# Decay rows repeated in DRAM and loaded by half heads, in a hybrid encoder layer

## The chip, the cores and the metric

The kernel runs on one core of a Trainium2 chip. The time is the device time of one execution in microseconds (us); for the kernel before the median of 3 runs is 810.5 us (810.26 to 810.57). One further execution was recorded by the hardware profiler; every duration below is of that execution. Engines are named as in the profile: PE is the TensorE matmul, PEld its weight load, DVE the VectorE, ACT the ScalarE, POOL the GpSimd, SP the SyncE, which here only issues transfers.

## The reference

One encoder layer in float32 over two sequences of 256 tokens, width 1024. From one joint projection come three branches: a bidirectional gated DeltaNet (8 heads, chunks of 64), a multi-head latent attention (MLA, 8 heads) and a cross-attention into a memory of 256 tokens. Each branch is gated and projected, the three are summed with sigmoid gates, projected and added to the input. The change works on the decay matrices of the first branch and on the order of work around them:

```python
gc = jnp.cumsum(g ..., axis=-1)                    # per head and direction
decay = jnp.exp(jnp.where(lower, gc[..., :, None] - gc[..., None, :], -jnp.inf))
lmat = jnp.einsum("nbhck,nbhek->nbhce", kb, kc) * decay * (1.0 - eye)
t_inv = lax.linalg.triangular_solve(lmat + eye, ...)
...
q_pe = _rope(q_pe, pos)
q_full = jnp.concatenate([q_nope, q_pe], axis=-1)
o_mla = _blocked_attention(q_full, k_full, v_mla, (D_NOPE + D_ROPE) ** -0.5)
```

So each head and each direction (forward, backward) needs exp(row of gc minus column of gc) under a triangular mask, times the products of the head's keys (kk), and then a triangular solve.

## The kernel before

Both sequences are handled together, as 512 columns. Each 128x128 block of a weight is used three times: weights and activations are split into a rounded part ("h": wh_, hh) and a remainder ("l": wl_, hl), and a product is hh·wh, hl·wh and hh·wl. A weight is therefore loaded (SP, L229, `wr_`), rounded (ACT, L241, `wh_`) and its remainder taken (DVE, L243, `wl_`) before PE can use all of it (L274). Two raw buffers and two of each part hold some two weights ahead.

There are three stages. In **front**, the memory branch and MLA run; between their products lie "fills", products that belong to other branches (the q, k, v of the DeltaNet `gm_qkv`, and its gates). In **middle**, a small planner (`weave`) puts the DeltaNet's heads among the remaining fills: it keeps a clock of PE time, each chain of work (heads coming in, two lanes of solves, heads going out, the norm) says with `yield cost, distance` how much PE time its step took and how much must pass before its next step, and fills take the time in between. PE follows the order that the planner wrote; DVE, ACT, POOL and SP get theirs from a scheduler with priorities. In **back** come the last projections. On each engine the order is fixed at build time: an instruction that waits holds up all behind it on that engine.

SP and ACT issue the transfers. As the built program shows, each transfer carries one of eight semaphores (DMAHW0 to DMAHW7), given out in turn over both engines, and a transfer waits until the one before it on the same semaphore has landed.

What the change touches:

- `d_r` (2 x 32 x 2 x 384 f32 in DRAM, L635 and L636): the rows of gc, for each direction, 4 rows per head. They are written in front.
- `decay_in` (L946): per head two tiles `e` of 128 x 768 (one per direction), each filled by four loads in which one row of `d_r` is repeated on 32 partitions: 8 loads per head, 64 in all. Two such buffers.
- `decay_mask` (POOL, L966) masks the triangles, four calls per head; `decay_exp` (ACT, L974) takes the exponent, eight calls per head; `gdn_in` makes the products kk (PE, L1008) and multiplies (DVE, L1018: `ne` from `e` and kk).
- `gdn_solve` goes through the triangular solve in steps that are 6.5 apart in the planner's time, `gdn_norm` multiplies by a row `rob` read back from DRAM (DVE, L1190) 10 after its load.
- `mla_rope` (called for half of MLA's heads at a time) rotates the position part of the queries on DVE, splits it, writes it to DRAM (L694, L695: `d_q`) and loads it back in another layout (L697, L700: `qs`). MLA's first product with it is `s_a<-ks,qs` (L335).
- In MLA, `pl_a` (DVE, L252) is the remainder of the transposed probabilities, `oa` (L370) the product with the values.

Of the kernel before, what the change touches and what calls it, by code (L numbers as in the profile page):

```python
# [7 lines left out]
F32 = mybir.dt.float32  # L8
# [173 lines left out]
class Layer:  # L182
    def __init__(self, tc, A):
        self.tc, self.nc, self.A = tc, tc.nc, A
# [39 lines left out]
    def weight(self, src, n, name, pool=None, into=None):  # L224
# [15 lines left out]
        with self.tc.high_priority(offset=60):  # L240
            self.wround = nc.scalar.activation(hi[:, :n], raw[:, :n], AF.Copy).ins  # L241
            lo = place("wl_", "wl")
            self.wsplit = nc.vector.tensor_tensor(lo[:, :n], raw[:, :n], hi[:, :n].bitcast(F32),  # L243
                                                  op=ALU.subtract).ins
        return hi, lo

    def split(self, src, hi, lo, scale=1.0):
# [3 lines left out]
        if isinstance(scale, float) and scale == 1.0:  # L251
            nc.vector.tensor_tensor(lo, src, hi.bitcast(F32), op=ALU.subtract)  # L252
# [72 lines left out]
    def attend(self, h, s, score, scale, vs, op, name):  # L325
# [39 lines left out]
        self.split(tp, hi, lo)  # L365
        n = 0
# [311 lines left out]
    def mla_rope(self, g):  # L678
# [6 lines left out]
        for j, (p1, p2, op) in enumerate(((pa, pb, ALU.subtract), (pb, pa, ALU.add))):  # L685
            t, u = self.tb("rt"), self.tb("ru")
# [5 lines left out]
            self.split(t, hi, lo)  # L692
# [8 lines left out]
        self.qs = qs1, qs2  # L701

# [237 lines left out]
    def decay_in(self, hh):  # L940
        es = []
        for d in range(2):
            e = self.pg.tile([P, 2, 384], F32, tag="e", bufs=2, name=f"e{hh}{d}")
            for a in range(4):
                src = self.d_r[d, 4 * hh + a:4 * hh + a + 1].rearrange("a s i -> a (s i)")
                self.nc.sync.dma_start(e[32 * a:32 * a + 32].rearrange("p s i -> p (s i)"), src.to_broadcast([32, 768]))  # L946
            es.append(e)
        return es
# [11 lines left out]
    def decay_mask(self, es):  # L960
        for d, e in enumerate(es):

            o = 128 if d else 0
            sg = -1 if d else 1
            for r in (slice(o, o + 128), slice(256, 384)):
                self.nc.gpsimd.affine_select(out=e[:, :, r], in_=e[:, :, r], pattern=[[0, 2], [sg, 128]],  # L966
                                             compare_op=ALU.is_ge, fill=NEG, base=0, channel_multiplier=-sg)

    def decay_exp(self, hh, d, e):
        for s in range(2):  # L970
            for cp in range(2):
                cch = cp if d == 0 else 1 - cp
                r = slice(0, 256) if cp == 0 else slice(256, 384)
                self.nc.scalar.activation(e[:, s, r], e[:, s, r], AF.Exp,  # L974
                                          bias=self.ngcl[:, d, 2 * s + cch, hh:hh + 1])

    def gdn_in(self, hh):
# [5 lines left out]
        es, vt = self.decay_in(hh), self.value_in(hh)  # L983
# [8 lines left out]
        yield 0.0, 10.0 if hh else 7.0  # L992
        self.decay_mask(es)
        for d in range(2):
            yield 0.0, 3.0
            with self.tc.issue_after(self.wround):
                self.decay_exp(hh, d, es[d])
        yield 0.0, 2.0
        v3 = vt.rearrange("p (t d) -> p t d", t=4)
        ne = pg.tile([P, 2, 2, 2, 384], F32, tag="ne", bufs=3, name=f"ne{hh}")  # L1000
        for s in range(2):
            pc = []
            hi, lo = hl[s]
            for cch in range(2):
# [5 lines left out]
                yield 0.65, 5.0 * cch  # L1010
            for d in range(2):
                for cp in range(2):
# [6 lines left out]
                        ne[:, :, d, s, r], es[d][:, s, r].unsqueeze(1).to_broadcast([P, 2, n]),  # L1019
                        cc[:, d, w:w + 1], kin, ALU.mult, ALU.mult)  # L1020
        nc.gpsimd.tensor_tensor(v3, v3, nk[:, 4 * h:4 * h + 4].unsqueeze(2).to_broadcast([P, 4, P]), op=ALU.mult)  # L1021
# [3 lines left out]
    def gdn_solve(self, hh):  # L1025
# [72 lines left out]
        for cp in range(2):  # L1098
            if cp == 1:
# [11 lines left out]
                yield 0.9, 6.5  # L1111
# [9 lines left out]
            yield 0.45, 6.5  # L1121
# [8 lines left out]
            yield 0.45, 6.5  # L1130
# [7 lines left out]
            yield 0.45, 6.5  # L1138
# [43 lines left out]
    def gdn_norm(self, hh):  # L1182
# [5 lines left out]
        yield 0.0, 6.0 if hh == 7 else 10.0  # L1188
# [506 lines left out]
```

## Time and profile before

| | before |
|---|---|
| median of 3 runs | 810.5 us |
| profiled execution, its own time | 810.69 us |
| span in the profile, first to last instruction | 808.9 us |
| mean granted PE clock | 0.998 |
| PE busy | 793.3 us, 98% |
| PEld busy | 699.5 us, 86% |
| DVE busy | 567.0 us, 70% |
| ACT busy | 448.9 us, 55% |
| POOL busy | 146.2 us, 18% |
| SP's queue of transfers, share of 16 DMA engines | 44.9% |
| ACT's queue of transfers | 0.8% |

Busy times are sums over instructions; the span is what counts, and 1.8 us of the execution's time lie outside it. The page divides the span into 40 slices, follows the chain of work that ended last, and groups instructions by line. The list of waits says, per engine, for what its instructions stood idle; the timeline gives single instructions with the idle time ahead of them in brackets and what ended it; a table of windows gives each engine's busy time within a stretch.

### The profile page before, as it was taken

The numbers are of one execution on the slowest core, as the hardware profiler recorded it, in microseconds if no ns is written. First come the engines' busy times: TensorE is split into PE (matmuls) and PEld (weight loads), VectorE is DVE, ScalarE is ACT, GpSimd is POOL, SyncE is SP. The second block draws the span as 40 slices with busy tenths as digits, with TensorE's granted clock in tenths as the row PEclk, the third lists the DMA queues.
The fourth block names the chain that finished last, engine by engine and source line by source line (L and its number), as shares of the span: only waits on it lengthen the run. The fifth ranks groups of instructions, "written<-read, shape, count | busy, mean of one in ns | idle before, by whom it ended". The sixth has DMA issues, their size and how long they took to land.

```text
span 808.9 us, 13180 instructions
## 1 busy us (share of the span) xinstructions
PE 793.3 (98%) x4822; PEld 699.5 (86%) x4822; DVE 567.0 (70%) x957; ACT 448.9 (55%) x895; POOL 146.2 (18%) x135
## 2 busy tenths in 40 slices
PE   9999999999999999999999999999999999999996
PEld 7888898889898889988888888788888888888885
DVE  7796358687699999668599998767644654455543
ACT  6765455456565566647666657576655552222332
POOL 0200111000010002074031137213110002223221
PEclk9999999999999999999999999999999999999999
DMA  8422222552417525355334454747444557354532
GB/s 324 170 75 103 92 87 72 183 158 72 118 59 221 173 95 161 130 157 158 130 111 130 140 147 154 203 137 192 135 132 131 182 188 262 128 196 147 186 104 105
DMA packets 68913, 118.20 MB, mean 146 GB/s; under 512 B 23664, under 2 KB 31216, under 8 KB 68848
## 3 DMA queue, kind: packets, MB, share of 16 engines
q1 hardware_dynamic: 67552, 115.00, 44.9%
q10 hardware_dynamic: 1296, 2.36, 0.8%
q8 instruction: 38, 0.62, 0.3%
q14 instruction: 27, 0.22, 0.1%
HBM read 98.24 MB, written 19.09 MB: 145 GB/s over the span
## 4 chain that ended last, share of the span: by engine, by line
PE 87%; DVE 6%; DMA 3%; ACT 2%; issue 1%; SPq 0%; POOL 0%; DVEq 0%; POOLq 0%; ACTq 0%
PE gm_g L274 15%; PE gm_qkv L274 13%; PE gm_z L274 7%; PE gm_bm L274 5%; PE gm_za L274 5%; PE y L1321 4%; PE gm_be L274 3%; PE gm_qm L274 3%; PE gm_km L274 3%; PE gm_bg L274 3%; PE o L1158 2%; PE gm_bg L1288 2%; PE kk L1008 2%; PE vm L426 2%; PE gm_qn L274 2%; PE gm_cq L274 2%
## 5 line engine op out<-in xcount | busy, mean ns | idle before, releaser
L775 DVE SCALAR_TENSOR_TENSOR kq<-cz,prm,kq 128x510 f32<-128x510 f32 (+1 forms) x64 | 52.7, 823 | 3.8 <-ACT kq L768 2.9
L274 PE MATMUL gm_qkv<-hh,wh_qkv 128*128 128x512 f32 x192 | 48.0, 384 | 1.3 <-ACT wh_qkv L241 1.3
L274 PE MATMUL gm_g<-hh,wl_g 128*128 128x512 f32 x192 | 48.9, 385 | 0.0
L274 PE MATMUL gm_g<-hh,wh_g 128*128 128x512 f32 x192 | 48.6, 386 | 0.0
L274 PE MATMUL gm_qkv<-hl,wh_qkv 128*128 128x512 f32 x192 | 48.1, 384 | 0.0
L274 PE MATMUL gm_g<-hl,wh_g 128*128 128x512 f32 x192 | 47.8, 384 | 0.0
L274 PE MATMUL gm_qkv<-hh,wl_qkv 128*128 128x512 f32 x192 | 47.4, 383 | 0.0
L243 DVE TENSOR_TENSOR wl_g<-wr_g,wh_g 128x1024 fp32r<-128x1024 f32 x24 | 29.5, 1227 | 19.6 <-PE gm_g L274 10.7
L243 DVE TENSOR_TENSOR wl_qkv<-wr_qkv,wh_qkv 128x1024 fp32r<-128x1024 f32 x24 | 30.7, 1281 | 16.4 <-PE gm_qkv L274 6.4
L1018 DVE SCALAR_TENSOR_TENSOR ne<-e,cc,kk 128x512 f32<-128x512 f32 (+1 forms) x64 | 35.5, 608 | 8.7 <-PE kk L1008 6.1
L274 PEld LDWEIGHTS gm_qkv<-hh,wh_qkv 128*128 128x128 f32 x192 | 35.6, 190 | 6.2 <-ACT wh_qkv L241 1.7
L274 PEld LDWEIGHTS gm_qkv<-hh,wl_qkv 128*128 128x128 f32 x192 | 36.0, 189 | 4.8
L274 PEld LDWEIGHTS gm_g<-hl,wh_g 128*128 128x128 f32 x192 | 35.7, 189 | 4.7
L274 PEld LDWEIGHTS gm_qkv<-hl,wh_qkv 128*128 128x128 f32 x192 | 35.7, 190 | 4.7
L274 PEld LDWEIGHTS gm_g<-hh,wl_g 128*128 128x128 f32 x192 | 35.4, 190 | 4.5
L274 PEld LDWEIGHTS gm_g<-hh,wh_g 128*128 128x128 f32 x192 | 35.2, 190 | 4.4
L1321 PE MATMUL y<-wh_wo,mh 128*128 128x512 f32 (+1 forms) x144 | 37.8, 356 | 0.0
L1263 POOL TENSOR_TENSOR mg<-mg,lg 128x512 f32<-128x512 f32 x16 | 28.0, 1761 | 50.6 <-DVE lg L1262 29.1
L241 ACT ACTIVATE wh_g<-wr_g 128x1024 fp32r<-128x1024 f32 x24 | 25.3, 1055 | 20.2 <-PE gm_g L274 13.8
L241 ACT ACTIVATE wh_qkv<-wr_qkv 128x1024 fp32r<-128x1024 f32 x24 | 25.4, 1057 | 19.7 <-PE gm_qkv L274 4.9
L990 POOL TENSOR_TENSOR kl<-kq,kh 128x512 fp32r<-128x512 f32 x16 | 22.6, 1418 | 53.3 <-ACT kh L988 50.7
L1021 POOL TENSOR_TENSOR vs<-vs,ns 128x512 f32<-128x512 f32 x8 | 8.4, 1049 | 127.1 <-DVE rs_a L352 84.9
(453 smaller groups left out, 2189.5 us busy)
## 6 DMA issues: line engine op xcount, KB each, us to landing
wr_g<-in_w_dram SPq DMA_DIRECT2D x24, 512.0 KB
wr_qkv<-in_w_dram SPq DMA_DIRECT2D x24, 512.0 KB
e<-d_r SPq DMA_DIRECT2D x64, 96.0 KB
wr_z<-in_w_dram SPq DMA_DIRECT2D x12, 512.0 KB
d_g<-gt_g SPq DMA_DIRECT2D x16, 256.0 KB
wr_za<-in_w_dram SPq DMA_DIRECT2D x8, 512.0 KB
lg<-d_g SPq DMA_DIRECT2D x16, 256.0 KB
wr_bm<-in_w_dram SPq DMA_DIRECT2D x8, 512.0 KB
```

The source lines that it names most:

```text
L241: self.wround = nc.scalar.activation(hi[:, :n], raw[:, :n], AF.Copy).ins
L243: self.wsplit = nc.vector.tensor_tensor(lo[:, :n], raw[:, :n], hi[:, :n].bitcast(F32), op=ALU.subtract).ins
L274: nc.tensor.matmul(pairs(ps[:m]), a[:, k * m:(k + 1) * m], turns(xs[k][j]), start=n == 0, stop=n == 3 * nk - 1)
L426: nc.tensor.matmul(pairs(vps[tb]), ms[k][a][:, t], turns(b[:, :512]), start=k == 0 and i == 0, stop=k == 7 and i == 2)
L775: nc.vector.scalar_tensor_tensor(ys, zs, self.cw[:, f, m:m + 1], ys, ALU.mult, ALU.add)
L990: nc.gpsimd.tensor_tensor(lo, src, hi.bitcast(F32), op=ALU.subtract)
L1008: nc.tensor.matmul(pairs(ps), a[:, k], turns(b), start=i == 0, stop=i == 2)
L1018: nc.vector.scalar_tensor_tensor(ne[:, :, d, s, r], es[d][:, s, r].unsqueeze(1).to_broadcast([P, 2, n]), cc[:, d, w:w + 1], kin, ALU.mult, ...
L1158: nc.tensor.matmul(out, ub[:, d, s, cp], rhs, start=n == 0, stop=n == 3)
L1263: nc.gpsimd.tensor_tensor(self.merged[d], self.merged[d], gt, op=ALU.add)
L1288: nc.tensor.matmul(pairs(ps), a[:, k * P:(k + 1) * P], turns(self.xg[k][j]), start=n == 0, stop=False)
L1321: nc.tensor.matmul(pairs(ps), xs[2 * j + q][a][:, t], turns(b[:, q * 512:(q + 1) * 512])[:, c0 // 2:c1 // 2], start=j == 0 and n == 0, sto ...
```

## The change

1. **Rows repeated in DRAM.** A new DRAM tensor `d_e` (2 x 8 x 128 x 2 x 384 f32) holds each head's four rows, each repeated 32 times. `decay_rows` fills it with 16 transfers from DRAM to DRAM, two per head, issued on ACT's queue. In the code it stands in the loop over MLA's heads.
2. **Tiles of half a head.** `e` becomes 128 x 384, one per head, sequence and direction: 32 loads of 192 KB in place of 64 of 96 KB, and four buffers in place of two (the same memory). Loads, masks and exponents become planner chains of their own (`decay_loads`, `decays`), half a head ahead of the products. The mask of a tile is one call on two blocks; their number per head stays four, that of the exponents eight.
3. **Distances.** From one kk to the next 5.0 becomes 6.5; the steps of the solve 6.5 to 7.2; the norm's row 10 to 12.
4. **MLA's rotation in two.** `mla_rope` becomes a generator: the first half of the rotation is made where all of it was, the second later, between the query products that follow; its split is put after the last weight rounding ahead of it in the program.
5. **One weight held back.** At the start of middle, the first weight remainder (`wl_`) is put after the last `pl_a` on DVE (`self.hold`).
6. Part 1 of the `xa` tiles moves from the e buffers to others and is loaded from another point on; the `xe` loads move one fill earlier.

The number and kind of PE's products stay as they are.

```diff
@@ weight
-            self.wsplit = nc.vector.tensor_tensor(lo[:, :n], raw[:, :n], hi[:, :n].bitcast(F32),
-                                                  op=ALU.subtract).ins
+            with nullcontext() if self.hold is None else self.tc.issue_after(self.hold):
+                self.wsplit = nc.vector.tensor_tensor(lo[:, :n], raw[:, :n], hi[:, :n].bitcast(F32),
+                                                      op=ALU.subtract).ins
+            self.hold = None
...
@@ mla_rope
         for j, (p1, p2, op) in enumerate(((pa, pb, ALU.subtract), (pb, pa, ALU.add))):
+            if j:
+                yield
...
-            self.split(t, hi, lo)
+            with self.tc.issue_after(self.wround) if j else nullcontext():
+                self.split(t, hi, lo)
...
+    def decay_rows(self, h):
+
+        src = self.d_r[:, 4 * h:4 * h + 4].rearrange("d a s i -> d a (s i)")
+        for d in range(2):
+            self.nc.scalar.dma_start(self.d_e[d, h].rearrange("(a b) s i -> a b (s i)", a=4),
+                                     src[d].unsqueeze(1).to_broadcast([4, 32, 768]))
+
+    def decay_in(self, hh, s):
         es = []
         for d in range(2):
-            e = self.pg.tile([P, 2, 384], F32, tag="e", bufs=2, name=f"e{hh}{d}")
-            for a in range(4):
-                src = self.d_r[d, 4 * hh + a:4 * hh + a + 1].rearrange("a s i -> a (s i)")
-                self.nc.sync.dma_start(e[32 * a:32 * a + 32].rearrange("p s i -> p (s i)"), src.to_broadcast([32, 768]))
+            e = self.pg.tile([P, 384], F32, tag="e", bufs=4, name=f"e{hh}{s}{d}")
+            self.nc.sync.dma_start(e, self.d_e[d, hh, :, s])
...
@@ gdn_in
-                yield 0.65, 5.0 * cch
+                yield 0.65, 6.5 * cch
...
@@ gdn_solve, four times
-                yield 0.9, 6.5
+                yield 0.9, 7.2
...
@@ gdn_norm
-        yield 0.0, 6.0 if hh == 7 else 10.0
+        yield 0.0, 6.0 if hh == 7 else 12.0
...
@@ front
+                self.decay_rows(4 * g + h)
                 with self.tc.high_priority(offset=50):
                     self.mla_attn(4 * g + h, z[0], *cur)
...
@@ middle
+    def decay_loads(self):
+        for n in range(16):
+            while n > self.e_done + 1:
+                yield 0.0, 0.5
+            self.e_raw[n] = self.decay_in(n // 2, n % 2), self.now + 8.0
+            yield 0.0, 0.5
...
-                hi, lo = (self.pg.tile([P, 512], F32R, tag="e", bufs=2, name=f"xa{f}") for _ in range(2))
+                hi, lo = self.s2(f"xa{f}h", F32R), self.pg.tile([P, 512], F32R, tag="t32", bufs=1, name=f"xa{f}l")
```

How the built program places it, at three points.

**ACT, in front, after `d_r` is written.** Before, this stretch of ACT is weight rounding (`wh_`), splits (`vh`, `rh`, `kn`) and steps of the convolution (`cz`, `kq`):

```order
L241 ACTIVATE wh_qkv_1702<-wr_qkv_1700 128x1024
L250 ACTIVATE vh_1680<-v_1673 128x512
L241 ACTIVATE wh_qn_1743<-wr_qn_1741 128x384
L250 ACTIVATE kn_1697<-gm_kn_1690 128x512
L241 ACTIVATE wh_qkv_1763<-wr_qkv_1761 128x1024
L776 ACTIVATE cz_1653<-kq_1652 128x512
```

Now (line numbers are those of the changed kernel; L951 is the transfer in `decay_rows`; the brackets give the semaphores waited for):

```order
L951 DMA d_e<-d_r 128x1x768 [waits DMAHW5_49]
L951 DMA d_e<-d_r 128x1x768 [waits DMAHW7_49]
L773 ACTIVATE cz_1639<-gm_qkv_1613 128x512 [waits PE_49,Pool_49]
L783 ACTIVATE cz_1570<-kq_1569 128x512 [waits DVE_49,Activation_49]
L951 DMA d_e<-d_r 128x1x768 [waits DMAHW1_49]
L241 ACTIVATE wh_qkv_1703<-wr_qkv_1701 128x1024 [waits PE_49]
L775 ACTIVATE kq_1638<-cz_1639,prm 128x2x256 [waits Activation_49]
L252 ACTIVATE vh_1666<-v_1659 128x512 [waits PE_49]
L951 DMA d_e<-d_r 128x1x768 [waits DMAHW3_49]
L951 DMA d_e<-d_r 128x1x768 [waits DMAHW5_49]
```

All 16 transfers stand within 29 rows of ACT, the first right behind the first weight that is rounded after `d_r` is issued, and none later in the loop over the heads; these rows hold the 12th to the 16th. Weights, splits and convolution steps stand between and behind them, and all but two of the 16 wait for the landing of an earlier transfer.

**SP, the same place.** Rows of SP behind the first two `qs` loads, after the change:

```order
L229 DMA wr_qn_1742<-in_w_dram 128x384 [waits DMAHW1_49,DMAHW2_49,DVE_49,Activation_49]
L706 DMA qs_1522<-d_q 32x2x512 [waits DMAHW7_49,DMAHW4_49]
L706 DMA qs_1522<-d_q 32x2x512 [waits DMAHW6_49]
L229 DMA wr_qkv_1762<-in_w_dram 128x1024 [waits DMAHW7_49,DVE_49]
L700 DMA d_q<-rh_1691 128x512 [waits DMAHW0_49]
L701 DMA d_q<-rl_1692 128x512 [waits DMAHW1_49]
L229 DMA wr_kn_1802<-in_w_dram 128x256 [waits DMAHW2_49,DVE_49]
L703 DMA qs_1521<-d_q 32x4x512 [waits DMAHW3_49,DMAHW0_49]
L703 DMA qs_1521<-d_q 32x4x512 [waits DMAHW4_49]
L706 DMA qs_1522<-d_q 32x2x512 [waits DMAHW5_49,DMAHW1_49]
L706 DMA qs_1522<-d_q 32x2x512 [waits DMAHW6_49]
L229 DMA wr_za_1819<-in_w_dram 128x1024 [waits DMAHW7_49,DVE_49]
```

Read with ACT's list in the order in which the semaphores are given out, the `d_e` transfers (counted 1 to 16) hold these of SP: `wr_qn` waits for the 9th, `wr_qkv_1762` for the 13th, the second `d_q<-rl` for the 14th, the third `qs_1521` for the 15th (DMAHW3), and `qs_1522` in the row with DMAHW5 for the 16th. `wr_za` stands behind it.

**DVE, at the end of MLA.** Before:

```order
L252 TENSOR_TENSOR pl_a_3653<-pt_a_3647,ph_a_3652 128x512
L243 TENSOR_TENSOR wl_qkv_3829<-wr_qkv_3825,wh_qkv_3827 128x1024
L252 TENSOR_TENSOR pl_a_3691<-pt_a_3685,ph_a_3690 128x512
L775 SCALAR_TENSOR_TENSOR kq_3733<-cz_3734,prm,kq_3733 128x2x255 x2
L757 TENSOR_TENSOR za_3589<-za_3589,oa_3623 128x512
```

and now:

```order
L254 TENSOR_TENSOR pl_a_3670<-pt_a_3664,ph_a_3669 128x512
L254 TENSOR_TENSOR pl_a_3708<-pt_a_3702,ph_a_3707 128x512
L244 TENSOR_TENSOR wl_g_3805<-wr_g_3801,wh_g_3803 128x1024
L244 TENSOR_TENSOR wl_qkv_3845<-wr_qkv_3841,wh_qkv_3843 128x1024
L782 SCALAR_TENSOR_TENSOR kq_3750<-cz_3751,prm,kq_3750 128x2x255
```

The last `pl_a` now stands ahead of both weight remainders.

More of the change, by code (lines that the diff above doesn't have):

```diff
@@ L183, in __init__ @@
     def __init__(self, tc, A):
-        self.tc, self.nc, self.A = tc, tc.nc, A
+        self.tc, self.nc, self.A, self.hold = tc, tc.nc, A, None
     def pool(self, st, name, space=None, **kw):
@@ L365, in attend @@
         self.split(tp, hi, lo)
+        self.plast = self.lsplit
         n = 0
@@ L701, in mla_rope @@
         self.qs = qs1, qs2
+        yield
     def mla_v(self, g):
@@ L961, in decay_mask, with decay_exp @@
         for d, e in enumerate(es):
[L963 to L975, printed above, removed]
+            e3 = e.rearrange("p (b i) -> p b i", b=3)
+            e3, sg = (e3[:, 1:3], -1) if d else (e3[:, 0:3:2], 1)
+            self.nc.gpsimd.affine_select(out=e3, in_=e3, pattern=[[0, 2], [sg, 128]],
+                                         compare_op=ALU.is_ge, fill=NEG, base=0, channel_multiplier=-sg)
+    def decay_exp(self, hh, s, d, e):
+        for cp in range(2):
+            cch = cp if d == 0 else 1 - cp
+            r = slice(0, 256) if cp == 0 else slice(256, 384)
+            self.nc.scalar.activation(e[:, r], e[:, r], AF.Exp, bias=self.ngcl[:, d, 2 * s + cch, hh:hh + 1])
     def gdn_in(self, hh):
@@ L991, in gdn_in @@
             hl.append((hi, lo))
[L992 to L998, printed above, removed]
+        yield 0.0, 4.0
         v3 = vt.rearrange("p (t d) -> p t d", t=4)
@@ L1003, in gdn_in @@
             hi, lo = hl[s]
+            while (hh, s) not in self.es:
+                yield 0.0, 0.5
+            es = self.es[hh, s]
             for cch in range(2):
@@ L1384, in run @@
             self.d_r = dp.tile([2, 32, 2, 384], F32, name="d_r")
+            self.d_e = dp.tile([2, 8, P, 2, 384], F32, name="d_e")
             self.d_om = dp.tile([P, 4, 512], F32, name="d_om")
@@ L1487, in front @@
         self.mem_attn(3, *q)
-        self.mla_rope(0)
+        rope = self.mla_rope(0)
+        next(rope)
         for g in range(2):
@@ L1491, in front, with between @@
             self.mla_v(g)
-            nxt = self.mla_qk(4 * g, lambda: fills(1))
+            def between():
+                next(rope)
+                fills(1)
+            nxt = self.mla_qk(4 * g, between)
             for h in range(4):
@@ L1506, in front @@
                 if h == 3 and g == 0:
-                    self.mla_rope(1)
+                    rope = self.mla_rope(1)
+                    next(rope)
                     fills(1)
@@ L1517, in middle @@
         nc = self.nc
-        fills = self.fills
+        self.hold = self.plast
         self.ym = []
@@ L1543, in preps, with decays @@
         self.pr[1] = yield from self.gdn_prep(1)
+    def decay_loads(self):
[3 more added lines that the diff above has]
+            self.e_raw[n] = self.decay_in(n // 2, n % 2), self.now + 8.0
+            yield 0.0, 0.5
+    def decays(self):
+        for n in range(16):
+            while n not in self.e_raw or self.now < self.e_raw[n][1]:
+                yield 0.0, 0.5
+            es, (h, s) = self.e_raw[n][0], (n // 2, n % 2)
+            self.decay_mask(es)
+            yield 0.0, 2.0
+            with self.tc.issue_after(self.wround):
+                for d in range(2):
+                    self.decay_exp(h, s, d, es[d])
+            yield 0.0, 2.5
+            self.es[h, s] = es
     def heads_in(self):
@@ L1572, in can @@
         if f == self.load_xa:
-            return (7 in self.hd, 7 in self.hd, 7 in self.hd, self.out > 5, 7 in self.started)[a[0]]
+            return (7 in self.hd, 5 in self.ub and 7 in self.started, 7 in self.hd, self.out > 5, 7 in self.started)[a[0]]
         if f == self.load_xe:
```

20 lines of the change are left out of this document (10 added, 10 removed).

## The prediction

> **What bounds the kernel now.** I read the page first, for the engine that is busy and the chain that ended last.
>
> ```profile
> span 808.9 us, 13180 instructions
> PE 793.3 (98%) x4822; PEld 699.5 (86%) x4822; DVE 567.0 (70%) x957; ACT 448.9 (55%) x895; POOL 146.2 (18%) x135
> q1 hardware_dynamic: 67552, 115.00, 44.9%
> PE 87%; DVE 6%; DMA 3%; ACT 2%; issue 1%; SPq 0%; POOL 0%; DVEq 0%; POOLq 0%; ACTq 0%
> ```
>
> PE is busy for 98% of the span and makes up 87% of the chain. The change leaves its products as they are, so it can only win what PE stands idle, and it can lose wherever it makes PE wait. What PE waits for is in the list of waits (total, times, longest):
>
> ```profile
> PE kk L1008 <- DVE ne L1018: 3.2, 3, 1.7
> PE zp L394 <- DVE zero L391: 1.5, 1, 1.5
> PE gm_qkv L274 <- ACT wh_qkv L241: 1.3, 1, 1.3
> PE oa L370 <- DVE pl_a L252: 1.1, 1, 1.1
> PE vm L426 <- ACT wh_vm L417: 0.5, 1, 0.5
> PE s_m L335 <- ACT p_m L349: 0.5, 1, 0.5
> PE gm_kn L274 <- DVE wl_kn L243: 0.3, 1, 0.3
> ```
>
> `zp` is the start, `vm` and `s_m` belong to the memory branch; the change touches none of them. The rest, 3.2 + 1.3 + 1.1 + 0.3 = 5.9 us, is what it can win at most: 0.7% of the time.
>
> Then I looked at the timeline around each of these, and at the place where the built program puts the new transfers, behind the writing of `d_r`.
>
> ```profile
> 147.88 0.59 SPq L636 DMA_DIRECT2D d_r<-rps  x1
> 150.71 0.69 DVE L521 TENSOR_TENSOR ru<-rb,sin 128x512 f32<-128x512 f32 x1 [5.42 <-DMA d_r<-rps]
> 161.72 0.91 SPq L697 DMA_DIRECT2D qs<-d_q  x2
> 162.94 0.77 SPq L700 DMA_DIRECT2D qs<-d_q  x2
> 163.19 2.00 PE L274 MATMUL gm_qkv<-hh,wh_qkv 128*128 128x512 f32 x8 [1.28 <-ACT wh_qkv L241]
> 170.41 1.89 PE L274 MATMUL gm_qkv<-hh,wh_qkv 128*128 128x512 f32 x8
> 171.16 0.33 SPq L229 DMA_DIRECT2D wr_za<-in_w_dram  x1
> 174.72 1.07 ACT L241 ACTIVATE wh_za<-wr_za 128x1024 fp32r<-128x1024 f32 x1 [2.30 <-DMA wr_za<-in_w_dram]
> 176.14 0.39 PE L335 MATMUL s_a<-ks,qs 128*128 128x256 f32 x2
> 178.00 1.24 PE L274 MATMUL gm_za<-hh,wh_za 128*128 128x512 f32 x5
> ```
>
> These are, in order: the last row of `d_r` issued, and landed by 150.71, 2.2 us after its issue ended; the `qs` loads; MLA's first product that needs them at 176.14; and the weight `wr_za`, issued at 171.16, landed at 174.72 (3.6 us later), used by PE from 178.00 on. The same place in a table of windows, beside the start of the kernel, where the DMA engines are fullest:
>
> ```profile
> core 0: us, PE busy (x) PEld busy (x) DVE busy (x) ACT busy (x) POOL busy (x), PEclk, DMA share, GB/s
> 0.00:20.00 20.00, 17.99 (x68) 14.59 (x69) 15.48 (x26) 13.89 (x24) 0.33 (x5) 1.00 0.90 324
> 150.00:176.00 26.00, 24.45 (x113) 20.78 (x112) 22.20 (x33) 13.12 (x23) 0.00 (x0) 1.00 0.60 182
> ```
>
> **The change, part by part.** All of it against the profiled execution's 810.7 us (1.8 of it outside the span; the median of the runs is 0.2 lower, which I leave out).
>
> *Copies from DRAM to DRAM: size.* Each of the 16 moves 128 rows of 768 f32, 393,216 bytes. The start moved 324 GB/s with 16 engines at a share of 0.90, so one engine gives 324 / (16 x 0.90) = 22.5 GB/s while it works. A copy spread over all 16 engines takes 393,216 / (16 x 22.5e9) = 1.09 us, all of them 17.5 us. But source and destination are not cut alike: the destination has 128 rows outermost, the source four (each repeated 32 times inside, a stride of nothing). A share of work that has to hold on both sides cannot be finer than the coarser of them unless it cuts inside its outermost step, and then only four engines work: 4 x 22.5 = 90 GB/s, 4.37 us a copy, 69.9 us for all. No row shows a large transfer of this form: the weights (128 rows on both sides) and the old `e` loads (32) are the nearest, and both divide by 16. So the bounds are 17.5 and 69.9 us with an engine's rate as at the start, and twice the latter, 139.8, if reading and writing DRAM halve the rate of an engine. I take 69.9 for the reason given.
>
> [...]
>
> *Copies: what waits.* They could lie beside PE if nothing queued behind them. But as the order rows show, ACT issues all of them at once when `d_r` has landed, at 150.7, and the transfers of SP and ACT share eight semaphores in turn: the weight `wr_qn` waits for the 9th copy, `wr_qkv` for the 13th, the `qs` loads for the 15th and 16th, and `wr_za` stands behind these on SP. On ACT, which keeps its order, the rounding of `wh_qkv` waits behind the 14th copy, itself waiting for the 8th. PE has its next weights only two ahead, so it stops when they stop. The 16th copy lands at 150.7 + 69.9 = 220.6. The same four engines also carry a share of what SP loads meanwhile: the window 150 to 176 had a DMA share of 0.60, 15.6 us of each engine's time. Between nothing and 15.6 I take a third, 5.2, since much of it waits for copies and so runs behind them: 225.8. Two `qs` issues (0.77 by their row) and then `wr_za` with its 3.6 us to landing and 1.07 of rounding give 231.2, against 178.00 before: +53.2. By `qs` alone it is 225.8 + 0.4 + 2.2 = 228.4 against 176.14, +52.3, so both roads meet. **Term: +53**, from +48 (nothing shared) to +63 (all of it). The 1.3 and 0.3 us of idle at 163 lie inside this stretch and are no gain of their own.
>
> If only the 13th copy counted (the later `qs` loads early enough), `wr_qkv` would land at 150.7 + 13 x 4.37 + 3.6 = 211.1, be rounded by 212.2, and its product, at 170.41 before, be 41.8 late: the low end of this term.
>
> *ACT's issues.* The nearest rows of one issue:
>
> ```profile
> L516 ACTq DMA_DIRECT2D d_om<-sp_om x4: 326/326/327, 83.2 to 147.6; - x4
> L946 SPq DMA_DIRECT2D e<-d_r x64: 303/419/857, 350.1 to 592.3; - x64
> ```
>
> 16 x 0.33 to 0.67 (twice the shortest; the longest `e` issue took 0.86) = 5.2 to 10.7 us, in a stretch where ACT works 13.12 of 26. With a stall of 50 us around it this costs nothing; without the stall it is 0 to 3 us of PE, since weights queue behind it.
>
> *Loads of `e`.* 64 issues of 0.42, 26.8 us of SP, become 32 of the plain form at about 0.33 (`d_om`), 10.6. The bytes stay. SP is not on the chain (SPq 0%), and the masks' wait for `e` stands on POOL, busy 18%; the exponents and masks keep their number. Nothing, and nothing if this cover went, since a load comes half a head ahead.
>
> *The held weight.* The stall of 1.1 us in `oa`:
>
> ```profile
> 348.48 1.23 DVE L243 TENSOR_TENSOR wl_qkv<-wr_qkv,wh_qkv 128x1024 fp32r<-128x1024 f32 x1 [3.53 <-PE gm_qkv L274]
> 349.62 0.68 DVE L252 TENSOR_TENSOR pl_a<-pt_a,ph_a 128x512 fp32r<-128x512 f32 x1
> 350.36 0.38 PE L370 MATMUL oa<-pl_a,vh 128*128 128x256 f32 x1 [1.13 <-DVE pl_a L252]
> ```
>
> `pl_a` waited behind a remainder of 1.23 us; now it stands ahead of it. The weights that wait instead are needed only after the product now running (eight matmuls of 1.9 us thrice). **Term: -1.1.**
>
> *Distances.* Two of the three waits for `ne` make up most of it, at 479 and 517; here they are, and what DVE did ahead of the second:
>
> ```profile
> 479.48 0.46 PE L1008 MATMUL kk<-kh 128*128 128x512 f32 x1 [1.33 <-DVE ne L1018]
> 512.62 0.69 DVE L1190 TENSOR_TENSOR og<-og,rob 128x512 f32<-128x512 f32 x1 [3.06 <-DMA rob<-d_n]
> 513.82 1.14 DVE L1018 SCALAR_TENSOR_TENSOR ne<-e,cc,kk 128x512 f32<-128x512 f32 x2
> 516.41 1.13 DVE L1018 SCALAR_TENSOR_TENSOR ne<-e,cc,kk 128x256 f32<-128x256 f32 x2
> 517.68 0.46 PE L1008 MATMUL kk<-kh 128*128 128x512 f32 x1 [1.68 <-DVE ne L1018]
> ```
>
> DVE stood 3.06 us at `og` for a row that had not come, `ne` behind it, and kk behind `ne` for its bank. With 12 instead of 10 of distance and 6.5 between the kk, I take two thirds of the 3.2: **-2.2** (0 to -3.2). Solves that step 7.2 apart end later, but other products fill the gaps, and the last output of a head keeps its place in PE's order; 0, up to +2 if the fills run out.
>
> *Rotation in two*, `xa`, `xe`: they move DVE work within the stalled stretch or loads that are awaited much later; 0.
>
> Sum: 810.7 + 53.2 - 1.1 - 2.2 = 860.6, said as **860 us**. The likeliest case's own range is 848 (the 13th copy decides, waits all gone) to 880 (all traffic shared, no gain from the distances).
>
> **Rivals.**
>
> *A. The copies use all 16 engines.* Then the last lands at 150.7 + 17.5 = 168.2, with sharing some 5 us later, and `qs` at about 175, just ahead of 176.14; ACT's issues fit into its 12.9 idle us. The gains stand, with half of the 1.6 at 163: 810.7 - 3.3 - 0.8, and 0 to 2 for late weights: **807**, clearly faster. For it: every transfer seen runs at such rates. Against it: the four rows of the source. This is the case on the other side, and it decides from the point where the 16th copy lands before some 173. Chance 0.20.
>
> *B. As A, but ACT's queue takes the gain back.* Ten us of issues in front of `wh_qkv`, which PE already awaits by 1.3 us at 163, cost 3 to 5 us: **811**. For it: that wait is there now, and weights stand behind every group of copies. Against it: ACT is half idle. Chance 0.08, three quarters of it within 0.2% of the time before, the rest slower.
>
> *C. Four engines, each at half its rate*, as every byte is read from and written to DRAM: 139.8 us, so 150.7 + 139.8 = 290.5, 70 later than in the forecast: **926**. For it: no row has DRAM on both sides. [...] Chance 0.07.
>
> **How the numbers follow.** The forecast has 0.65. Beyond 880 lie C and about 0.05 of it, below 806 a third of A: so 806 to 880 leaves out under 0.2. A comparison of this kernel can tell about 0.2% (1.6 us) from no change. Faster: A, 0.20. Same: three quarters of B, 0.06. Slower: the forecast, C and the rest of B, 0.74.
>
> **What would show it.** Right: PE idle for some 50 us between 155 and 235, its waits ending on ACT's `wh_qkv`, on `wr_qkv` and `wr_za`, and on `qs`; the issues of `d_e` on ACT about 4.4 us apart from the sixth on; a DMA share of about a quarter in that stretch, since four of 16 engines work; behind it the same order of PE, every piece some 50 us later, with no wait of `oa` for `pl_a`. Wrong: a DMA share near 0.9 for 20 us after 150 and no gap on PE (A), PE waits of a few us for `wh_qkv` alone (B), copies some 9 us apart (C). If the copies are fast and the result is still slower, the reason lies in the distances, and kk or the lanes would wait longer than before.

## The result, and the profile after

The changed kernel takes 861.25 us (median of 4 runs, 860.71 to 862.68) against 810.38 for the kernel before: a ratio of 1.0621, 95% interval 1.0604 to 1.0637. The forecast was 860. The page of the changed kernel, the rows that answer to those of before (busy times, ACT's queue of transfers, the chain by engine):

```profile
PE 800.6 (93%) x4822; PEld 700.8 (82%) x4822; DVE 567.4 (66%) x957; ACT 448.1 (52%) x895; POOL 152.2 (18%) x135
q10 hardware_dynamic: 3408, 8.65, 2.6%
PE 75%; DMA 8%; DVE 7%; ACT 3%; ACTq 3%; issue 2%; POOL 2%; SPq 0%; POOLq 0%; DVEq 0%
```

PE has the same 4822 products, but is busy for 93% of the span, and its share of the chain fell from 87 to 75%; most of that went to transfers and to their issue on ACT (DMA 3 to 8%, ACTq 0 to 3%; POOL, DVE, ACT and issue have the rest). From PE's list of waits (total, times, longest):

```profile
PE gm_kn L276 <- ACT wh_kn L241: 22.4, 1, 22.4
PE gm_qkv L276 <- ACT wh_qkv L241: 12.3, 2, 10.7
PE gm_qn L276 <- ACT wh_qn L241: 4.4, 1, 4.4
PE s_a L337 <- DMA qs<-d_q: 3.1, 2, 2.6
PE us L1140 <- DVE w L1135: 2.3, 1, 2.3
PE xs L1131 <- ACT u L1123: 1.2, 2, 1.1
PE kk L1013 <- DVE ne L1023: 1.1, 3, 0.4
PE gm_za L276 <- ACT wh_za L241: 1.0, 1, 1.0
PE xs L1131 <- ACT ub L1126: 0.7, 1, 0.7
PE oa L373 <- DVE pl_a L254: 0.3, 1, 0.3
```

The roundings of three kinds of weight and the `qs` loads make up 42 us of idle time (of which 1.3, for `wh_qkv`, was there before). The timeline of the changed kernel shows why they are late: ACT with its issues (ACTq), SP, and PE.

```profile
157.78 4.74 ACTq L951 DMA_DIRECT2D d_e<-d_r  x1
162.60 3.60 ACTq L951 DMA_DIRECT2D d_e<-d_r  x1
166.27 15.18 ACTq L951 DMA_DIRECT2D d_e<-d_r  x4
181.54 0.42 ACT L241 ACTIVATE wh_kn<-wr_kn 128x256 fp32r<-128x256 f32 x1 [14.71 <-issue]
182.01 1.22 PE L276 MATMUL gm_kn<-klh,wh_kn 128*128 128x512 f32 x2 [22.41 <-ACT wh_kn L241]
195.64 3.78 PE L276 MATMUL gm_qkv<-hh,wh_qkv 128*128 128x512 f32 x8 [10.70 <-ACT wh_qkv L241]
220.14 0.77 SPq L706 DMA_DIRECT2D qs<-d_q  x2
221.01 0.38 SPq L229 DMA_DIRECT2D wr_za<-in_w_dram  x1
222.08 0.35 PE L337 MATMUL s_a<-ks,qs 128*128 128x256 f32 x1 [2.58 <-DMA qs<-d_q]
225.91 1.99 PE L276 MATMUL gm_za<-hh,wh_za 128*128 128x512 f32 x8 [1.02 <-ACT wh_za L241]
```

Four issues that take 0.59 us each where nothing holds them (the shortest of the 16) hold ACT for 15.18 us, because each waits on a semaphore for a copy that has not landed; 15.18 / 4 = 3.8 us is the pace of the copies. `wh_kn`, whose weight had been issued at 144, stands behind them, and PE behind `wh_kn` for 22.4 us. On SP the `qs` loads waited for copies three times, 30.2 us in all, the longest 21.4. The windows of this stretch (length, busy times, granted PE clock, DMA share, GB/s):

```profile
155.00:160.00 5.00, 4.60 (x22) 3.69 (x20) 2.13 (x4) 0.00 (x0) 0.00 (x0) 1.00 0.61 231
160.00:163.00 3.00, 0.00 (x0) 0.00 (x0) 0.00 (x0) 0.43 (x1) 0.00 (x0) 0.99 0.26 103
166.00:180.00 14.00, 0.00 (x0) 0.00 (x0) 1.35 (x2) 0.60 (x1) 0.00 (x0) 0.50 0.31 118
180.00:196.00 16.00, 3.29 (x7) 2.15 (x8) 2.10 (x4) 3.52 (x6) 0.00 (x0) 0.50 0.35 126
```

While PE stands still the DMA engines are busy for 0.26 to 0.35 of their time: about four of 16, at some 100 to 130 GB/s. That is no lack of work, and less than the DMA engines move elsewhere: 324 GB/s over the first 20 us of the kernel before, and 231 in the first row above.

To see where the time goes along the program, I follow three products through all kernels: the first `gm_za` of MLA, the last `oa` that waits for `pl_a` (end of front), and the first product of the output, `y`. The last is read from the row of its line, before and after:

```profile
L1321 PE MATMUL y<-wh_wo,mh x144: 272/379/380, 760.1 to 801.5; 128*128 128x512 f32 x112, 128*128 128x256 f32 x32
...
L1327 PE MATMUL y<-wh_wo,mh x144: 273/379/379, 810.9 to 852.3; 128*128 128x512 f32 x112, 128*128 128x256 f32 x32
```

| kernel | median, us | first `gm_za` | last `oa` | first `y` | from `oa` to `y` |
|---|---|---|---|---|---|
| before | 810.38 | 178.00 | 350.36 | 760.1 | 409.7 |
| changed | 861.25 | 225.91 | 397.51 | 810.9 | 413.4 |
| wide | 825.82 | 192.07 | 363.81 | 775.0 | 411.2 |
| eight | 831.85 | 197.32 | 368.86 | 781.2 | 412.3 |
| later | 827.75 | 177.72 | 364.39 | 776.5 | 412.1 |
| wide_later | 822.29 | 177.05 | 358.78 | 771.4 | 412.6 |
| poolq | 829.59 | 187.29 | 365.14 | 778.4 | 413.3 |
| direct | 818.96 | 178.09 | 349.04 | 769.1 | 420.1 |
| wide_dist | 827.04 | 190.74 | 362.45 | 776.2 | 413.8 |
| dist | 812.07 | 178.08 | 350.14 | 760.7 | 410.6 |
| hold_kk | 815.60 | 177.92 | 349.81 | 765.5 | 415.7 |
| rope_hold | 808.73 | 177.93 | 349.13 | 758.4 | 409.3 |
| hold | 809.05 | 177.61 | 350.03 | 759.2 | 409.2 |
| best | 810.52 | 177.61 | 348.56 | 763.4 | 414.8 |

Of the 50.8 us at `y`, 47.9 stand at `gm_za`, 47.2 at the end of front, and 3.7 come in the middle. (The three points are of one profiled execution each, which differs from the median by up to a few us; where these differ by one or two, only the ratios below decide. Each ratio below is against runs of the kernel before that were made beside it, with medians of 810.3 to 810.8.)

### The profile page after: what moved, and what is told of

Its sections match the earlier page's. It is cut to its first block, busy times and chain, and to the rows that moved or that the text cites. A ratio compares the mean times of both kernels' runs of the same rounds, so it can differ in the third digit from the quotient of the medians.

```text
span 859.1 us, 13151 instructions
## 1 busy us (share of the span) xinstructions
PE 800.6 (93%) x4822; PEld 700.8 (82%) x4822; DVE 567.4 (66%) x957; ACT 448.1 (52%) x895; POOL 152.2 (18%) x135
## 4 chain that ended last, share of the span: by engine, by line
PE 75%; DMA 8%; DVE 7%; ACT 3%; ACTq 3%; issue 2%; POOL 2%; SPq 0%; POOLq 0%; DVEq 0%
PE gm_g L276 13%; PE gm_qkv L276 10%; PE gm_z L276 5%; PE gm_bm L276 5%; DMA d_e<-d_r 4%; PE gm_za L276 4%; PE y L1327 4%; ACTq L951 3%; PE gm_be L276 2%; PE gm_qm L276 2%; PE gm_km L276 2%; PE gm_bg L276 2%; PE gm_bg L1294 2%; PE vm L429 2%; PE o L1164 2%
## 5 line engine op out<-in xcount | busy, mean ns | idle before, releaser
L244 DVE TENSOR_TENSOR wl_g<-wr_g,wh_g 128x1024 fp32r<-128x1024 f32 x24 | 31.3, 1306 | 23.2 <-ACT wh_g L241 11.3
L998 POOL TENSOR_TENSOR kl<-kq,kh 128x512 fp32r<-128x512 f32 x16 | 25.6, 1604 | 50.6 <-ACT kh L996 50.6
L983 ACT ACTIVATE e<-e,ngcl 128x256 f32<-128x256 f32 x64 | 24.4, 443 | 16.8 <-POOL e L976 16.8
```

The lines of the kernel that those rows point to most:

```text
L983: self.nc.scalar.activation(e[:, r], e[:, r], AF.Exp, bias=self.ngcl[:, d, 2 * s + cch, hh:hh + 1])
L998: nc.gpsimd.tensor_tensor(lo, src, hi.bitcast(F32), op=ALU.subtract)
```

## The experiments

My theory: a copy with four source rows outermost runs on four of 16 engines, 16 of them queue up in one burst, and all that waits on ACT or on a shared semaphore behind them stops PE. Rivals: a copy with DRAM on both sides is slow in any form; the issues and semaphores cost the time whatever the copies take; the slow copies do harm wherever they stand.

### wide: the copy's outermost count, nothing else

```diff
-            self.nc.scalar.dma_start(self.d_e[d, h].rearrange("(a b) s i -> a b (s i)", a=4),
-                                     src[d].unsqueeze(1).to_broadcast([4, 32, 768]))
+            self.nc.scalar.dma_start(self.d_e[d, h].rearrange("(a b) s i -> b a (s i)", a=4),
+                                     src[d].unsqueeze(0).to_broadcast([32, 4, 768]))
```

> The changed kernel with one edit: source and destination of each of the 16 copies are walked with the 32 repeats outermost (32 x 4 x 768 on both sides) in place of the four source rows; the same bytes, the same order of instructions on every engine. Theory (the four rows outermost leave a copy on four of 16 engines): by the changed kernel's page ACT's queue took 2.6% of 16 engines where it took 0.8% before, about 254 us of engine time for 6.29 MB, 24.8 GB/s per engine; on 16 engines a copy takes 1.0 us, all of them 16 us, the last lands near 167 us, PE's gap between 160 and 226 shrinks from 48 us to 0 to 5, and with the 2 to 3 us that were lost in the middle the time is 810 to 818 us. Rival (a copy with DRAM on both sides is slow in any form): copies still some 4 us apart, 861 us. Rival (the eight shared semaphores and ACT's issues cost most of it): the gap stays above 15 us although the copies land fast, over 825 us.

Measured: 825.82 us (825.16 to 827.77), 1.0183 of before (1.0146 to 1.0219). The queue, the line of the copies (issue in ns, least, median, most; first and last) and windows of wide:

```profile
q10 hardware_dynamic: 3600, 8.65, 2.9%
```

```profile
L951 ACTq DMA_DIRECT2D d_e<-d_r x16: 536/536/623, 148.6 to 171.2; - x16
```

```profile
150.00:160.00 10.00, 10.00 (x47) 8.50 (x45) 8.99 (x14) 3.33 (x6) 0.00 (x0) 1.00 0.80 264
160.00:170.00 10.00, 5.32 (x18) 3.85 (x18) 4.43 (x7) 4.20 (x7) 0.00 (x0) 0.83 1.04 369
170.00:180.00 10.00, 5.99 (x22) 4.67 (x21) 6.82 (x11) 2.85 (x5) 0.00 (x0) 0.81 0.84 304
```

With the same bytes and the same order of every engine's instructions, the last issue falls at 171.2 in place of 201.3, the DMA share between 160 and 170 is 1.04 in place of 0.26, and `gm_za` is 33.8 us earlier. The engine time of the copies stayed nearly as it was: ACT's queue took (2.6% x 859.1 - 0.8% x 808.9) x 16 = 254 us in the changed kernel and 278 by the same sum in wide (the page rounds its shares, which leaves some 5% open). So a copy is not slow on an engine; it had too few of them. The rival of DRAM on both sides falls. But the time lies above my 810 to 818: 14 us of delay stay at `gm_za`. It is just above the 825 that I had given to the rival of semaphores and issues; but these can't cost most of the loss, since 35 of 51 us came back with the same issues and semaphores. Of the 14.1 us, PE idles for 7.7; the other 6.4 are nearly the same products running slower (from 150 to `gm_za` PE is busy for 32.85 us, and for 26.45 in the kernel before), at the granted clocks of 0.83 and 0.81 in the rows above.

### eight: twice the outermost count, half the copies

```diff
+        if h % 2:
+            return
-        src = self.d_r[:, 4 * h:4 * h + 4].rearrange("d a s i -> d a (s i)")
+        src = self.d_r[:, 4 * h:4 * h + 8].rearrange("d a s i -> d a (s i)")
         for d in range(2):
-            self.nc.scalar.dma_start(self.d_e[d, h].rearrange("(a b) s i -> a b (s i)", a=4),
-                                     src[d].unsqueeze(1).to_broadcast([4, 32, 768]))
+            self.nc.scalar.dma_start(self.d_e[d, h:h + 2].rearrange("h (a b) s i -> (h a) b (s i)", a=4),
+                                     src[d].unsqueeze(1).to_broadcast([8, 32, 768]))
```

> The changed kernel with copies for two heads at a time: 8 transfers with eight source rows outermost, 786 KB each, the same bytes in all. Theory of the outermost count: eight engines at 24.8 GB/s take 4.0 us a copy, 32 us in all, the last lands near 183 to 188 us, and what needs it (qs, wr_za) comes 8 to 14 us late: 819 to 828 us. Rival (slow for DRAM on both sides): twice the time a copy, half as many, the stall as before, about 855 to 861 us. Rival (the number of transfers in the queue counts): half the transfers, so half the stall, about 835 us.

Measured: 831.85 us, 1.027 (1.0221 to 1.0318). It lies between wide and the changed kernel, as by the count of engines (4, 8, 16: `gm_za` 47.9, 19.3 and 14.1 us late), but above my 819 to 828, and near the 835 that I had given to the number of transfers, which the time alone doesn't exclude. The DMA share does: while PE stands still (162 to 170) it is 0.52, at 209 GB/s, where the changed kernel has 0.26 at 104 (163 to 173), so twice the engines move twice the bytes; and wide, with 16 transfers, is faster than eight with 8. What my figure left out is seen in wide, where the delay does not go to nothing either.

### later: the same slow copies, two per head

```diff
         for d in range(2):
-            self.nc.scalar.dma_start(self.d_e[d, h] ...
+          with self.tc.issue_after(self.wround):
+            self.nc.scalar.dma_start(self.d_e[d, h] ...
```

> The changed kernel with each pair of copies placed on ACT behind the last weight rounding ahead of it in the program, so two per head of MLA between 178 and 345 us in place of all 16 at 150; the form of a copy stays (four rows outermost). The order of PE moves a little with it. If the loss comes from 16 slow copies queued at once in front of weights and qs, a pair takes 8 us of each 18 to 20 us and little waits: 808 to 818 us, with a DMA share raised by a tenth over that stretch. If a slow copy costs wherever it stands (weights that share its four engines or its semaphore come 4 to 8 us late), each head loses 3 to 6 us: 835 to 860 us.

Measured: 827.75 us (822.81 to 829.26), 1.0192 (1.0144 to 1.024). `gm_za` is back at 177.72, so the 48 us at this place need both, the slow form and the burst. It then lost 14.3 until the last `oa`. One part is the slow form, seen in the timeline of later where a weight is issued just behind two copies:

```profile
326.05 0.61 ACTq L952 DMA_DIRECT2D d_e<-d_r  x1
326.70 0.60 ACTq L952 DMA_DIRECT2D d_e<-d_r  x1
328.61 0.42 SPq L229 DMA_DIRECT2D wr_g<-in_w_dram  x1
339.44 1.06 ACT L241 ACTIVATE wh_g<-wr_g 128x1024 fp32r<-128x1024 f32 x1 [6.62 <-DMA wr_g<-in_w_dram]
```

`wr_g` landed 10.8 us after its issue, where `wr_za` took 3.6 in the kernel before, and PE waited 3.9 us. The result lies between the two expectations.

### wide_later: both edits

The two diffs above together.

> Both edits together: copies with the 32 repeats outermost (wide) and two per head of MLA in place of all at once (later). The order of PE is that of later. later still lost 4.3 us at 282 and 4.1 at 340 to weights (wh_qkv, wh_g) and wide 13 us around 163 to 182. If the first come from copies of 4 us and the second from 16 copies in one burst, both vanish and what is left is the middle: 810.5 to 814 us. If a copy in front of a weight costs 4 us in any form, 822 to 828 us.

Measured: 822.29 us, 1.0147 (1.0133 to 1.0161). `gm_za` comes at 177.05: placed by heads and on all engines, the copies cost nothing there, and the wait for `wr_g` at 340 is gone. So the 14 us that wide had kept are the burst. But the time lies above my 810.5 to 814, and in the range that I had given to a copy that costs 4 us in any form: up to the last `oa` 8.4 us are still lost. The largest piece is a wait of 5.1 us for `wh_qkv` at 282; SP's rows in this kernel show its weight issued only behind the second half of the rotation's `qs`:

```profile
272.66 0.38 SPq L701 DMA_DIRECT2D d_q<-rl  x1
276.32 0.79 SPq L706 DMA_DIRECT2D qs<-d_q  x2
277.20 0.38 SPq L229 DMA_DIRECT2D wr_qkv<-in_w_dram  x1
281.21 1.06 ACT L241 ACTIVATE wh_qkv<-wr_qkv 128x1024 fp32r<-128x1024 f32 x1 [7.39 <-DMA wr_qkv<-in_w_dram]
```

In the kernel before the same weight was issued at 269. The weight landed in its usual time, some 3.6 us after its issue, and no copy was issued between 221 and 288 here, so it is not a copy that costs this. Moving the copies moved the order of SP and PE too; later has this wait as well (4.1 us), with the slow form, and poolq has one of 3 us at 288, long after its copies. I read it as a cost of the order; no run isolates it.

### poolq: the same copies from POOL's queue

```diff
-            self.nc.scalar.dma_start(self.d_e[d, h] ...
+            self.nc.gpsimd.dma_start(self.d_e[d, h] ...
```

> The changed kernel with the 16 copies issued by POOL in place of ACT: the same form (four source rows outermost), the same point in time, but POOL has eight semaphores of its own, so neither ACT's weights nor SP's qs and weights wait for a copy by a shared semaphore; they only share the DMA engines. Theory (the loss of 48 us is made by what queues behind the copies on ACT and on the shared semaphores): the gap at 160 to 226 falls to 0 to 6 us, 810 to 818 us, while the copies may take their 60 us. [...]

Measured: 829.59 us, 1.0236 (1.0223 to 1.0249). The time lies 11.6 us above the 818 of its theory, but the run did not test what it was made for. In poolq, the queue of these copies, their line, and the window of the burst:

```profile
q0 software_dynamic: 4352, 6.32, 2.3%
```

```profile
L951 POOL DMA_DIRECT2D d_e<-d_r x16: 680/681/889, 148.4 to 167.6; - x16
DMA to landing us min/median/max: 7.4/13.0/16.5
```

```profile
160.00:170.00 10.00, 7.26 (x25) 5.61 (x25) 6.96 (x11) 4.09 (x7) 3.62 (x6) 0.83 1.06 385
```

A copy took 13.0 us to land (the median), and yet up to eight were under way at once (POOL waited for an earlier copy at 8 of its 16 issues, 8.8 us in all), and the DMA share was 1.06: issued from POOL, these copies did not all stand on the same four engines (6.29 MB between 148 and 185 are 170 GB/s, where four engines at 24.8 give 99). So it is another case of a burst on 16 engines, now without a shared semaphore (in the built program POOL's copies carry eight of their own) and without a wait on ACT, and `gm_za` is still 9.3 us late. Beside wide's 14.1 this puts most of that loss to the sharing of the engines, and some 5 us to ACT and the semaphores; the split is a difference of two kernels whose orders differ a little.

### direct: no copies

```diff
-            self.nc.sync.dma_start(e, self.d_e[d, hh, :, s])
+            for a in range(4):
+                self.nc.sync.dma_start(e[32 * a:32 * a + 32], self.d_r[d, 4 * hh + a:4 * hh + a + 1, s].to_broadcast([32, 384]))
...
-                self.decay_rows(4 * g + h)
```

> The changed kernel without d_e: no copies; each half-head tile is loaded straight from d_r, one row repeated on 32 partitions as before (128 loads of 48 KB in place of 64 of 96 KB). All else of the change stays. Theory (the copies alone cause the front's loss): PE's gap between 160 and 185 us is gone and what is left is the rest of the change: about 1 us won at the last oa, 1.5 to 3 lost in the middle, nothing or 1.5 won at 163: 809.5 to 812.5 us. Rival (the split rotation and its later qs loads cause part of the front's loss): 814 to 820 us with a gap near 165 to 180. Rival (the loads' issues on SP now hurt, 128 of 0.42 us): waits of POOL and ne for e in the middle grow, 813 to 818 us.

Measured: 818.96 us, 1.0101 (1.0082 to 1.012). Front is as before to 0.1 us at `gm_za` and 1.3 ahead at the last `oa`: the copies alone cause the loss in front, the split rotation none of it. The middle lost 10.4, and the time is 1 us above the range of the third expectation, which had put such a loss to the 128 loads (32 in the changed kernel). The wait of POOL's masks for them does rise, from 32.2 us before to 49.5. The lines of direct:

```profile
L959 SPq DMA_DIRECT2D e<-d_r x128: 302/419/1365, 343.1 to 594.1; - x128
  POOL e L977: 49.5, 16
```

But that the loads make the loss is not shown: PE's wait of kk for `ne` fell to 1.7 us. Its longest wait in the middle is 2.7 us for `kd` at 408, for which the profile names no cause, and behind it the granted clock was 0.53 from 410 to 415. Of the loss, 5.6 us are idle time and 4.7 are longer products. So this kernel can't price the half-head tiles themselves.

### wide_dist and dist: the distances

wide_dist is wide, and dist the kernel before, each with its distances exchanged for the other's:

```diff
-                yield 0.65, 5.0 * cch
+                yield 0.65, 6.5 * cch
-                yield 0.9, 6.5
+                yield 0.9, 7.2
-        yield 0.0, 6.0 if hh == 7 else 10.0
+        yield 0.0, 6.0 if hh == 7 else 12.0
```

(as in dist; the other three solve steps alike, and the reverse in wide_dist).

> As wide, with the planner's distances of the kernel before (5.0 between key products, 6.5 between solve steps, 10 for the norm's row). If the wider distances are what cost the middle of the changed kernel its 2.8 us (us, xs and kk waited 5 us there), this is 2 to 4 us faster than wide. If the half-head tiles and their own chains are the cause, it is equal to wide within 1 us. If the distances do what they are for, it is 2 to 3 us slower than wide.

> The kernel before with the four wider distances alone (6.5 between key products, 7.2 between solve steps, 12 for the norm's row). From wide (middle 1.5 us longer than before, from the last oa on) against wide_dist (4.0 longer) the distances are worth 2.5 us there; if that carries over to full-head tiles: 807.2 to 808.6 us, the waits of kk for ne (3.2 us) down to about 1. If they only help the half-head tiles: 809.8 to 811.5 us.

Measured: wide_dist 827.04 us, 1.0192 (1.0154 to 1.023), not told apart from wide, though its one profile has 2.6 us more from `oa` to `y`. dist 812.07 us, 1.0025 (1.0012 to 1.0038): slower than before and above both of my ranges. In dist the waits for `ne` fell from 3.2 to 1.4 as I had reckoned, but the last solves came late, after the fills had run out: the last kk starts at 647.7 in place of 630.0, the last `u` at 685.4 in place of 678.5 (waits, and the two rows of PE):

```profile
PE kk L1008 <- DVE ne L1018: 1.4, 3, 0.8
PE u L1115 <- ACT y L1092: 0.7, 1, 0.7
PE gm_bm L274 <- ACT xa L250: 0.6, 1, 0.6
```

```profile
665.37 0.68 PE L1115 MATMUL u<-vs,y 128*128 128x128 f32 x4 [0.75 <-ACT y L1092]
674.23 1.64 PE L274 MATMUL gm_bm<-xa,wh_bm 128*128 128x512 f32 x6 [0.58 <-ACT xa L250]
```

In this profile (811.14 us, below dist's median) the new waits are no longer than what was saved; hold_kk, next, shows what can make such waits dearer.

### hold_kk: key products wider, solve steps not, and the held weight

> The kernel before with the held weight and the wider distances of the key products (6.5) and of the norm's row (12), the solve steps left at 6.5. In dist the waits of kk for ne fell by 1.8 us, but the last solves came late and cost 2 to 3 us at 660 to 675. If the solve steps did the latter and the key products the former: 0.8 + 1.8 less, 807.0 to 808.6 us, and no waits of xs and u at 660. If the key products push the last solves out by themselves: 809.5 to 811 us.

The edit is that of dist without its solve steps (6.5 stays), with that of hold below. Measured: 815.60 us, 1.0056 (1.0042 to 1.007), slower than before and than dist, and 4 us above both of my ranges. No wait for `ne` is left at all, and new ones stand in its place (waits, and two windows around the first):

```profile
PE u L1118 <- DVE vs L1113: 2.5, 1, 2.5
PE gm_z L276 <- DVE zt_z L1203: 2.2, 1, 2.2
```

```profile
665.00:670.00 5.00, 2.84 (x40) 2.38 (x40) 3.21 (x8) 4.04 (x14) 1.01 (x1) 0.62 0.97 338
670.00:675.00 5.00, 5.00 (x26) 4.81 (x26) 0.84 (x2) 2.21 (x7) 0.00 (x0) 0.69 0.95 344
```

The first of these lies at 667, where the last head's solve now comes later (the last `u` at 690.2) and has little to hide behind. The spacing of the key products, with that of the norm's row, pushes the last solves out without that of the solve steps; my pair of causes was wrong. And the waits are the smaller part of the loss. Of the 6.0 us from `oa` to `y`, 1.7 are idle time; 4.3 are longer products (PE is busy for 410.9 us there, and for 406.6 before), since the granted clock fell at each of the two waits: around the first it is 0.50 from 666.3 to 673 (0.62 and 0.69 are means over 5 us), and behind the second, at 566.63, eight matmuls of `gm_z` take 3.14 us, where eight of `gm_g` at 580.11 take 1.89.

### hold, rope_hold and best: the parts that might help

hold has the held weight alone, rope_hold also the rotation in two, best also the distances of dist; their edits are those of the change.

> The kernel before with the held weight and the rotation in two, nothing else. The two act at different places, so one trace shows both: the held weight takes PE's wait for pl_a at 350 from 1.1 to 0.3 us (as in all runs of the change), 0.8 won; the rotation takes the wait for wh_qkv at 163 (1.3 us) away if the bunch of rotation work was its cause: 808.0 to 808.6 us. If the wait at 163 has another cause, 809.3 to 809.7.

> The kernel before with the held weight, the rotation in two and the wider distances: all of the change but the repeated rows in DRAM and the tiles of half a head (and the moves of xa and xe). If the parts add: 0.8 + 0 to 1.4 + 2.5 us less, 805.6 to 807.2 us. If the distances were only of use for half-head tiles: 808 to 809.7.

> The kernel before with the held weight alone. In rope_hold the wait of PE for wh_qkv at 163 stayed at 1.3 us and the rows of DVE around it stayed in their order, so the rotation in two should be worth nothing: then this is equal to rope_hold, 808.6 to 809.6 us (0.8 of it at the last oa). If the rotation in two wins something elsewhere (in rope_hold PE was 0.3 us ahead at 268 us), this is 0.3 to 1 us slower than rope_hold, 809.3 to 810.3.

Measured: hold 809.05 us, 0.9983 (0.9967 to 0.9999), as in its first range; rope_hold 808.73, 0.9975 (0.9964 to 0.9986), between its two; best 810.52, 1.0003 (0.9988 to 1.0018), above both of its ranges. PE's waits in rope_hold:

```profile
PE gm_qkv L276 <- ACT wh_qkv L241: 1.3, 1, 1.3
PE oa L373 <- DVE pl_a L254: 0.3, 1, 0.3
```

The held weight does what it says, 1.1 to 0.3 us. The rotation in two leaves the wait for `wh_qkv` at 163 as it was: 1.3 us before, 1.3 now. hold and rope_hold are not told apart. At the first `y` their profiles are 0.9 and 1.7 us ahead of the kernel before, of which the shorter wait for `pl_a` explains 0.8. With the distances added, the gain is gone; in best's profile (3 us above its median) the clock falls to half at 666, behind waits of 1.1 and 0.8 us of the last solves (the longest `u` takes 551 ns there, the median 275). rope_hold is the fastest that was run, 2 us below the kernel before and 52 below the changed one.

## Why the prediction was right, and where not

**What bounds the kernel, and where it would stall**: right. PE idled between 160 and 226, on `wh_kn`, `wh_qkv`, `wh_qn`, `qs` and `wh_za`, all named (`wh_qn` by its load, `wr_qn`) but `wh_kn`, which stands in the same queue on ACT. The DMA share was about a quarter, as for four engines, and the copies 3.8 us apart.

**Four engines**: right, and shown by wide, which changed only the form, and by eight, whose DMA share doubled. No row of before shows a copy of this form; that it stands on four engines was my argument from the cut of its two sides, and the runs bear it out: with 4 and 8 rows outermost the DMA share is 0.26 and 0.52 while PE stands still, with 32 it is 1.04 over 160 to 170, and `gm_za` is 47.9, 19.3 and 14.1 us late. For copies issued from POOL no run shows on how many engines one stands; in poolq the same form took 13.0 us a copy, up to eight at once, at a share of 1.06.

**An engine's rate**: mis-sized. I took 22.5 GB/s from the start of the kernel; 6.29 MB in 254 us of engine time are 24.8, so all copies take 63.5 us on four engines, not 69.9. The share of other traffic was about right: 150.7 + 63.5 = 214.2, and the `qs` loads that wait for the 16th copy were issued at 220.1, 5.9 later against my 5.2. With `wr_za` landing 3.4 us after its issue ended, `gm_za` came at 225.9 and not at 231.2: the term of +53.2 measured +47.9.

**The gains behind it**: the held weight was worth 0.8 of 1.1. The distances were forecast at -2.2, and the middle measured +3.7 (409.7 to 413.4). What the -2.2 stood for came: the waits of kk for `ne` fell from 3.2 to 1.1. The step that failed is that nothing else would wait longer, "other products fill the gaps" with its 0: `us` waited 2.3 us for DVE at 536, and `xs` 1.9 us for ACT at 556 to 635, all of it idle time that was not there before. It does not lie where dist and hold_kk lose, for in the changed kernel PE is never idle from 640 to `y`. That the half-head tiles cost something of their own was not in my sum (their chains were put at nothing); wide_dist's 4.0 us with the old distances hint at it. Whether distances or tiles make the new waits no run separates, so the cause of the +3.7 stays open.

So two terms were off by 5 to 6 us each, in opposite directions, and that 860 meets 861 so closely is luck. The mechanism and its place were right, which is what the 0.65 was for.

**The rivals.** A (16 engines) is what wide would have been, and A was wrong too: at 16 engines the burst still cost 14 us, where I had allowed 0 to 2. I had reckoned that the last copy lands in time, but not that 6.3 MB of copies and the 4.7 MB that all loads moved between 150 and 176 before (182 GB/s x 26 us) are 11 MB, 29 us of all engines at the 385 GB/s seen in poolq; nor had I a term for products that run slower between the waits. B's reason, the wait on ACT, was part of it. C fell: at 24.8 GB/s an engine did not run at half of 22.5.

## What to carry to other kernels

Look at the outermost count of both sides of a transfer before its bytes: a broadcast with four rows outermost, issued from ACT, ran on four of 16 engines (a DMA share of 0.26), and putting the repeats outermost, with the same bytes and the same order of instructions, gave back 35 of 51 us. A transfer without a consumer nearby still held what stood behind it on its engine (ACT for 15.18 us) and on its semaphores (`qs` on SP for up to 21.4 us), and the scheduler may issue all of them at once as soon as their source is ready, so look where they land in the order, not where the code calls them. And with an engine 98% busy, widening a distance to remove a wait moved the wait, in dist, hold_kk and best, to the end of the chain, where nothing is left to cover it. A wait of PE can cost more than its length (in hold_kk 1.7 us of idle time came with 4.3 of longer products), so count how long its products take as well as how long it idles.

## What was not expected of the hardware

PE's granted clock was 0.99 from 160 to 163 and 0.50 from 163 to 196, after PE had stopped at 159.6, and products after the stall ran at half speed: eight matmuls of `gm_qkv` took 3.78 us at 195.64, where they took 1.89 at 152.96, at a clock of 1.00. Here it hid inside the stall. In wide, with gaps of 2 to 4 us, the clock was still 0.83 and 0.81 over 160 to 180, and 7.7 us of idle time came with 6.4 of longer products, so short gaps cost more than their length there. The clock fell behind such gaps elsewhere too: in hold_kk behind gaps of 2.2 and 2.5 us, and in best behind two gaps of 1.1 and 0.8 us close together. The gap of 2.3 us at 536 in the changed kernel did not lower it (1.00 from 532 to 540), so in these runs the length of one gap alone does not decide it.

Copies of one form and size came 3.8 us apart from ACT at a DMA share of 0.26, and took 13 us each from POOL, eight at a time and at a share of 1.06: here the queue decided the spread, not the form alone.
